# A second buffer for the delta heads' output gates, paid for by a pool of attention constants that ends with the attention

## The chip, the cores and the metric

The kernel runs on one core of a Trainium2 chip: TensorE (PE, with its weight loads PEld), VectorE (DVE), ScalarE (ACT), GpSimd (POOL) and SyncE (SP, which issues most DMAs). The metric is the time of one execution in microseconds, the median of the runs shown. The profile tells of one execution; its span runs from the first to the last instruction.

## The reference

One step of a decoder layer for a prompt of 1024 tokens and 8 single-token samples, in float32. What bears on the change is the gated delta rule with 8 heads of width 128, and its output gate:

```python
h = rmsnorm(x) * (1 + scale1) + shift1
qkv, gdn_gate, beta_raw, a_raw, sq, sk, sv, ga, gb = split(h @ w_in)
q, k, v = silu(causal_conv4(qkv))            # per head 128 wide; q, k normalized
for each chunk of the prompt:                # a chain through the state S
    v_new = u - w @ S
    o     = q_dec @ S + a_intra @ v_new
    S     = S * last + k_dec.T @ v_new
y_a = (rmsnorm(o) * w_norm * silu(gdn_gate)) @ w_gdn_out
y_b = sliding_window_attention(sq, sk, sv) @ w_swa_out
x   = x + gate1 * ((sigmoid(ga) * y_a + sigmoid(gb) * y_b) @ w_o)
x   = x + gate2 * ffn(rmsnorm(x))            # conv-gated feed-forward, 2816 wide
```

Here `u` and `w` come from the inverse of a unit triangular matrix for each chunk, which the kernel forms for each head with 128 tokens in a chunk. The silu(gdn_gate) of each head is the output gate of the title.

## The kernel before

**Stages.** The conditioning and the first norm, the sliding-window attention in four groups, the delta heads one after the other, the branches (`branches`, the output projections of attention and delta heads), and the feed-forward half. Activations lie with features on the partitions and the 1032 tokens along the free dimension, in three parts of 384, 384 and 264 columns. Every product of float32 matrices is made of three fast ones (`mm3`, L180 to L182: high by high, low by high, high by low), over eight steps of 128 features. So a projection of 128 columns for a part is 24 matmuls, and for all tokens 72.

**A delta head.** `run` starts head 0 and then goes through h = 0 to 7. For each h it weaves these streams: `unit_inverse(h)`, the blockwise inverse of head h (in five blocks of small matmuls: L1038, L1044, L1056, L1061, L1070 and, last, L1074, with copies on ScalarE and transposes on VectorE between them); `delta_scan(h)`, eight chunks, each with a chain of products with the key (L947), the inverse W (L950) and the decayed key (L954), between which lie y on VectorE (L948), s on ScalarE (L952) and the new state S on VectorE (L963); `delta_prepare(h + 1)`, transposes and Gram products (L190, L906, L907); and projections. Those are, for h up to 5, `delta_gate(h)` and after it `delta_project(h + 2)`, which makes K, Q and V of the head after the next with `conv_tile`: project, copy into a room z (L780), four taps on VectorE (L784, L786) and a silu (L791, L792). At h = 6 the gates of heads 6 and 7 come in their place.

`delta_gate(h)` projects 72 matmuls, takes the tanh of each part from PSUM on ScalarE (L858) and writes the gate on VectorE into `sg` (L859). The scan multiplies its normalized output into `sg` in two halves (L983) and sends it to DRAM as `oa` (L988). `sg` has one buffer, so the gate of a head can be written only when the output of the head before has left; head 7's takes a room z instead.

**Rooms that matter.** K and Q have three buffers (`bufs=3`), V has one, and z has two, one of them in the pool `pz` and one in `pa`. Projections use two banks of PSUM (`pmm`, tag mm), the filler a third one (`pmf`).

**Filler.** `gates` (the two branch gates, 16 tiles of 72 matmuls, evicted by ScalarE at L1294 into gt) and `early_out` (the attention's output projection for one part of the tokens, evicted at L1326 by VectorE with a gate that is loaded from DRAM at L1323) come in `pieces` of eight steps with a low priority. In the stages of heads 6 and 7 each filler step is also tied to a step of the scan (`spaced`). When the last gate is done, six loads of sample states (L1119, 512 KB each) use the room that it frees.

**What sets the order.** A scheduler places all instructions: `weave` and `later` give priorities, and a simulated timeline tells when an operand, a PSUM bank or a room is ready. Each engine then runs its instructions in that fixed order, and a later tile of a pool waits for the tiles that lay at its addresses.

**Pools.** `cp` holds the constants of the whole program, `cp2` those that last through the branches. `p2`, the attention's pool, ends with it, and `pgt`, `pz`, `pg`, `pa` and `p4` (which has `sg`) take the space then.

Of the kernel before, what the change touches and what calls it, by code (L numbers as in the profile page):

```python
# [18 lines left out]
P = 128  # L19
NP = 1024  # L20
NS = 8
NT = NP + NS
KC = 8
H = 8
# [9 lines left out]
HALF = [(0, 512), (512, 520)]  # L34
QW = 260
KEPT = {"ident", "ones", "mhalf", "phalf", "vecs", "fcw", "mT", "a2"}
COL_GATE, COL_BETA, COL_SQ = 3072, 4096, 4112
COL_SK, COL_SV, COL_GA, COL_GB = 5136, 5392, 5648, 6672

# [25 lines left out]
class Step:  # L65
# [28 lines left out]
        return pool.tile(shape, dt, tag=tag, name=f"{tag}_{self.n}", **kw)  # L94

    def const(self, shape, name, dt=F32):
        pool = self.cp if name in KEPT else self.cp2
        return pool.tile(shape, dt, tag=name, name=name)


# [749 lines left out]
    def delta_gate(self, pa, pool, h):  # L850

        nc = self.nc
        sg = self.t(pool, [P, NT], "sg", bufs=1) if h + 1 < H else self.t(self.pz, [P, NT + 3], "z")[:, :NT]

        def gate_out(t, ps):
            lo, n = PARTS[t]
            th = self.t(pa, [P, 512], "th", bufs=2)[:, :n]
            nc.scalar.activation(th, ps, AF.Tanh, scale=0.5)  # L858
            nc.vector.scalar_tensor_tensor(sg[:, lo:lo + n], th, 1.0, ps, op0=ALU.add, op1=ALU.mult)  # L859

        self.project(self.win(COL_GATE + h * P), self.h, gate_out)
        nc.gpsimd.tensor_copy(self.sgs[:, h, :], sg[:, NP:NT])
        self.sg[h] = sg
        yield
# [1086 lines left out]

    def run(self):
        S, nc = ExitStack, self.nc
        self.constants()
        with S() as ca:
            with S() as c:
                pool, psum = self.pool("p2", 1, ctx=c), self.pool("q2", 1, PSUM, ctx=c)
                for tag, bufs in dict(qst=8, raw=2, kh=2, kl=2, E=3, obt=2, pp=2, pc=2, o=2).items():
                    self.bufs[id(pool), tag] = bufs
                self.conditioning(pool, psum)  # L1960
                self.vectors(pool, psum)
                self.h = self.new_parts()
                self.a1 = self.const([P, KC, 9], "a1")
                for lo in (8, 0, 12, 4):
                    self.modulation(pool, psum, "sc", lo, (("qst", 8),), "mrows")
                    if lo == 8:
                        self.junk = self.t(pool, [P, NP], "vch", bufs=1)
                        xs = self.norm_part(pool, self.load_rows(pool, 0, ("raw", "raw", "V")))
                    if lo in (8, 12):
                        k = lo - 8  # L1970
                        self.norm_scale(self.a1[:, k:k + 4, :], lo, self.n1w[:, k:k + 4])
                    if lo == 0:
                        self.modulate_part(pool, psum, 0, xs, self.a1, 0, range(4))
                    if lo == 12:
                        self.early = [self.win(COL_SK)]
                    if lo == 4:
                        self.early.append(self.win(COL_SQ))
                with self.tc.issue_after(self.mod_load.ins):
                    self.early.append(self.win(COL_SV, tags=("wmh", "wml"), home=pool, raw=(pool, "qst", 8)))
                with self.tc.issue_after(self.w_load.ins):  # L1980
                    self.xs = {1: self.load_rows(pool, 1, ["qst"] * 3)}
                self.junk = self.t(pool, [P, NP], "qst", bufs=8)
                self.early.append(self.win(COL_SQ + P, tags=("obt", "obt"), home=pool))
                self.xs[2] = self.load_rows(pool, 2, ("raw", "raw", "V"))
                self.modulate_part(pool, psum, 0, xs, self.a1, 0, range(4, KC))
                self.attention(pool, psum)
# [6 lines left out]
            with S() as c:  # L1993
                pa, pool, psum = self.pool("pa", 1, ctx=c), self.pool("p4", 1, ctx=c), self.pool("q4", 1, PSUM, ctx=c)
# [27 lines left out]
        with S() as c:  # L2022
            pool2, pool = self.pool("p6b", 1, ctx=c), self.pool("p6", 1, ctx=c)
# [48 lines left out]
```

## Time and profile before

| | us |
|---|---|
| median of 3 runs | 2083.78 |
| lowest and highest | 2079.47, 2090.38 |
| span of the profiled execution | 2084.4 |
| PE busy | 2012.7 (97%) |
| DVE busy | 1347.8 (65%) |
| ACT busy | 900.2 (43%) |
| POOL busy | 520.2 (25%) |
| mean granted TensorE clock | 0.991 |

The profiled execution is known by its span alone, which holds what the times measure; it lies 0.6 us above the median. A row of the profile that groups instructions has the line, engine and operation, the written and read tiles, the count, then the busy time in us and the mean of one in ns, and last the idle time of the engine before them with what ended it. A row of a timeline has the start, the duration, the instruction and in brackets the idle time before it. A row of waits has who waited for whom, the total, how often and the longest. The attention ends at about 440 us, the delta heads at about 1110.

### The profile page before, as it was taken

The page shows a single profiled execution, that of the slowest core. Times are in us where ns is not written, and L with a number is a line of the kernel's source. Part 1 is how long each engine was busy: PE and PEld are TensorE (multiplying, and loading weights), DVE is VectorE, ACT ScalarE, POOL GpSimd, SP SyncE. Part 2 cuts the span into 40 slices and gives each one's busy share as a digit, 9 for nine tenths or more (in the row PEclk, how much of TensorE's full clock was granted, in tenths as well). Part 3 has the DMA queues.
Part 4 walks back from the last instruction along what each step waited for, and adds up shares of the span by engine and source line. Part 5 has one row for each costly group of instructions (what it writes and reads, how often), then busy time and mean ns, then how long its engine had stood idle before and what let it go on. Part 6 is the DMA issues. An engine that isn't in the chain of part 4 may idle for free.

```text
span 2084.4 us, 41297 instructions
## 1 busy us (share of the span) xinstructions
PE 2012.7 (97%) x16245; PEld 1910.2 (92%) x16245; DVE 1347.8 (65%) x2714; ACT 900.2 (43%) x2233; POOL 520.2 (25%) x594
## 2 busy tenths in 40 slices
PE   7999998999999999989989999999999999999897
PEld 4987877799999999989989999999999999999897
DVE  5755768473655647656544675578876776767756
ACT  4664545433344243432342542354444444534443
POOL 2000000121321221201111000005575466446421
PEclk9999999999999999999999999999999999999999
DMA  8256443331332322312275855323333333488862
GB/s 300 62 144 210 135 167 116 117 94 51 80 80 61 73 72 52 89 42 62 63 223 172 285 186 163 112 63 97 105 91 112 102 92 112 136 305 266 291 215 94
DMA packets 301887, 275.75 MB, mean 132 GB/s; under 512 B 59730, under 2 KB 248111, under 8 KB 301676
## 3 DMA queue, kind: packets, MB, share of 16 engines
q1 hardware_dynamic: 295642, 252.14, 39.6%
q0 software_dynamic: 5552, 20.37, 2.8%
q8 instruction: 127, 2.08, 0.4%
q14 instruction: 68, 0.56, 0.1%
q10 hardware_dynamic: 498, 0.61, 0.1%
HBM read 212.93 MB, written 62.51 MB: 132 GB/s over the span
## 4 chain that ended last, share of the span: by engine, by line
PE 83%; DVE 5%; DMA 5%; ACT 3%; issue 1%; SPq 1%; POOL 1%; DVEq 0%; POOLq 0%; ACTq 0%
PE mm L180 19%; PE mm L181 18%; PE mm L182 18%; PE wv L180 3%; PE wv L182 3%; PE wv L181 3%; PE wy L182 2%; PE wy L180 2%; PE wy L181 2%; PE pv L652 1%; PE pt L190 1%; PE tp L190 1%; DVE x L1472 1%; PE mm L264 1%; PE rc L954 1%
## 5 line engine op out<-in xcount | busy, mean ns | idle before, releaser
L180 PE MATMUL mm<-b1h,wh 128*128 128x384 f32 (+1 forms) x1520 | 496.9, 328 | 3.7 <-ACT gt L1294 1.6
L181 PE MATMUL mm<-b1l,wh 128*128 128x384 f32 (+1 forms) x1520 | 489.3, 323 | 0.0
L182 PE MATMUL mm<-b1h,wl 128*128 128x384 f32 (+1 forms) x1520 | 488.0, 323 | 0.3 <-DVE wl L130 0.3
L180 PEld LDWEIGHTS mm<-b1h,wh 128*128 128x128 f32 x1520 | 286.7, 189 | 12.4 <-issue 4.6
L181 PEld LDWEIGHTS mm<-b1l,wh 128*128 128x128 f32 x1520 | 287.1, 189 | 4.4 <-issue 3.1
L182 PEld LDWEIGHTS mm<-b1h,wl 128*128 128x128 f32 x1520 | 286.3, 189 | 3.9 <-issue 2.8
L129 ACT ACTIVATE wh<-raw 128x1024 fp32r<-128x1024 f32 x83 | 87.0, 1049 | 122.4 <-PE mm L181 70.2
L130 DVE TENSOR_TENSOR wl<-raw,wh 128x1024 fp32r<-128x1024 f32 x82 | 101.0, 1233 | 57.2 <-ACT wh L129 55.1
L181 PE MATMUL mm<-pk,w 128*128 128x260 f32 (+1 forms) x440 | 124.8, 284 | 1.1 <-DVE pk L130 1.1
L180 PE MATMUL mm<-pk,w 128*128 128x260 f32 (+1 forms) x440 | 124.8, 284 | 0.0
L182 PE MATMUL mm<-pk,w 128*128 128x260 f32 (+1 forms) x440 | 124.5, 283 | 0.0
L130 DVE TENSOR_TENSOR w<-ws,w 128x512 fp32r<-128x512 f32 x88 | 78.0, 886 | 36.9 <-ACT w L129 36.7
L1626 ACT COPY bml<-mm 128x256 f32<-128x256 f32 (+1 forms) x132 | 48.9, 371 | 100.6 <-PE mm L182 96.7
L180 PE MATMUL mm<-bmh,w 128*128 128x260 f32 (+1 forms) x320 | 90.3, 282 | 0.0
L182 PE MATMUL mm<-bmh,w 128*128 128x260 f32 (+1 forms) x320 | 90.1, 282 | 0.0
L1681 DVE SCALAR_TENSOR_TENSOR fa<-fz,fcw,fa 128x512 f32<-128x512 f32 x88 | 75.2, 874 | 18.2 <-ACT fa L1679 17.9
L180 PE MATMUL mm<-b2h,wh 128*128 128x384 f32 (+1 forms) x256 | 83.2, 328 | 2.9 <-ACT wh L129 2.8
L181 PEld LDWEIGHTS mm<-pk,w 128*128 128x128 f32 x440 | 83.2, 189 | 1.3 <-DVE pk L130 1.3
L181 PE MATMUL mm<-b2l,wh 128*128 128x384 f32 (+1 forms) x256 | 83.6, 327 | 0.4 <-DVE b2l L130 0.4
L180 PEld LDWEIGHTS mm<-pk,w 128*128 128x128 f32 x440 | 83.2, 189 | 0.2 <-ACT bml L1626 0.2
L182 PEld LDWEIGHTS mm<-pk,w 128*128 128x128 f32 x440 | 83.4, 190 | 0.0
L182 PE MATMUL mm<-b2h,wl 128*128 128x384 f32 (+1 forms) x256 | 82.8, 326 | 0.0
(645 smaller groups left out, 5886.2 us busy)
## 6 DMA issues: line engine op xcount, KB each, us to landing
raw<-in_w_in_dram SPq DMA_DIRECT2D x59, 512.0 KB
ws<-in_w_ffn_down_dram SPq DMA_DIRECT2D x55, 256.0 KB
raw<-xd SPq DMA_DIRECT2D x47, 258.0 KB
raw<-in_w_ffn_down_dram SPq DMA_DIRECT2D x47, 256.0 KB
raw<-in_w_ffn_gate_dram SPq DMA_DIRECT2D x22, 512.0 KB
raw<-in_w_ffn_up_dram SPq DMA_DIRECT2D x22, 512.0 KB
qst<-in_w_mod_dram SPq DMA_DIRECT2D x16, 512.0 KB
raw<-in_w_mod_dram SPq DMA_DIRECT2D x16, 512.0 KB
```

The source lines that it names most:

```text
L129: self.nc.scalar.activation(hi, x, AF.Copy)
L130: (eng or self.nc.vector).tensor_tensor(lo, x, hi.bitcast(F32), op=ALU.subtract)
L180: mm(ps, whi, xhi, start=first, stop=False, **kw)
L181: mm(ps, whi, xlo, start=False, stop=False, **kw)
L182: self.last_mm = mm(ps, wlo, xhi, start=False, stop=last, **kw).ins
L190: self.nc.tensor.transpose(out, in_, self.ident[:p, :p])
L264: nc.tensor.matmul(ps[32 * j:32 * j + 32], self.cT[:, k0 + j, :], ws[j // 2][:, j % 2, :], start=k0 == 0, stop=k0 > 0)
L652: nc.tensor.matmul(pv[64 * r:64 * r + 64], V[:, n - back, ch], ps[:, r::2, :], start=back == 0, stop=back == (n > 0))
L954: yield step(nc.tensor.matmul(ds, kd[:, n, :], s, start=True, stop=True))
L1472: nc.vector.scalar_tensor_tensor(x[:, :np_], ps[:, :np_], by[:, j, 8:9], x[:, :np_], op0=ALU.mult, op1=ALU.add)
L1626: self.last_copy = nc.scalar.copy(r[p, i], x[p])
L1681: nc.vector.scalar_tensor_tensor(ai[:, c:e], zi[:, j + c:j + e], col(j), ai[:, c:e], op0=ALU.mult, op1=ALU.add)
```

## The change

Ten constants that only the attention (and what runs beside it) reads go from `cp2` into a new pool `cp1`, opened inside the attention's scope and closed with it: four triangular masks, the sinks, four small tiles of sample queries and keys and values, and the modulation of the first norm. They make up 4.8 KB in each partition. `sg` gets two buffers of 4.1 KB, for all eight heads; head 7's gate no longer takes a room z. Constants are now made behind the opening of that pool.

```diff
 KEPT = {"ident", "ones", "mhalf", "phalf", "vecs", "fcw", "mT", "a2"}
+SHORT = {"triu", "tril", "trilu", "stril", "sink", "qs", "kx", "vx", "zero", "a1"}
...
     def const(self, shape, name, dt=F32):
-        pool = self.cp if name in KEPT else self.cp2
+        pool = self.cp if name in KEPT else self.cp1 if name in SHORT else self.cp2
...
     def delta_gate(self, pa, pool, h):
...
-        sg = self.t(pool, [P, NT], "sg", bufs=1) if h + 1 < H else self.t(self.pz, [P, NT + 3], "z")[:, :NT]
+        sg = self.t(pool, [P, NT], "sg", bufs=2)
...
     def run(self):
         S, nc = ExitStack, self.nc
-        self.constants()
         with S() as ca:
             with S() as c:
+                self.cp1 = self.pool("cp1", 1, ctx=c)
+                self.constants()
```

No instruction is added or taken away on any engine. The order stays as it was up to TensorE's work beside the inverse of head 1, and from the branches on it differs in few places. In between, each gate now stands a scan earlier. Three places show what else moved; line numbers of the changed kernel are one higher than the profile's (L1038 is L1039 there).

Place 1: TensorE at the end of head 4's scan, from its last chunk on. rc, o and S belong to the scan, tp to the inverse of head 5 and to the transposes for head 6; mm is a projection. Before (the key that is transposed is head 6's; the last mm is a piece of head 5's gate):

```order
L958 MATMUL o_9698<-s_9733,A_8916 128x128
L182 MATMUL mm_10286<-b1h_12_150,wl_10255 128x384
L947 MATMUL rc_9742<-S_9739,K_7325 128x128
L957 MATMUL o_9698<-S_9739,Q_7326 128x128
L950 MATMUL rc_9745<-y_9741,W_4535 128x128
L954 MATMUL rc_9749<-s_9747,kd_8864 128x128
L958 MATMUL o_9698<-s_9747,A_8916 128x128
L1074 MATMUL tp_10183<-W_4535,UZ_9991 64x64 x8
L190 MATMUL tp_10876<-ident,K_9341 128x128 x4
L190 MATMUL tp_10887<-ident,K_9341 128x128 x4
L190 MATMUL rc_9764<-ident,vn_8949 128x128 x4
```

Now (mm_10600 is the third part of the value projection of head 7; the filler stands behind it):

```order
L948 MATMUL rc_9746<-S_9743,K_7329 128x128
L958 MATMUL o_9702<-S_9743,Q_7330 128x128
L951 MATMUL rc_9749<-y_9745,W_4539 128x128
L955 MATMUL rc_9753<-s_9751,kd_8868 128x128
L959 MATMUL o_9702<-s_9751,A_8920 128x128
L1075 MATMUL tp_10187<-W_4539,UZ_9995 64x64 x8
L191 MATMUL tp_10880<-ident,K_9345 128x128 x4
L191 MATMUL tp_10891<-ident,K_9345 128x128 x4
L181 MATMUL mm_10600<-b1h_14_155,wh_10544 128x264
L182 MATMUL mm_10600<-b1l_15_156,wh_10544 128x264
L183 MATMUL mm_10600<-b1h_14_155,wl_10545 128x264
```

What moved: head 7's value projection now stands here, behind the key transposes; before, it came in the scan of head 5. On VectorE the same place, from the last y of head 4's scan on. Now (K_10347 and Q_10348 are those of head 7):

```order
L949 SCALAR_TENSOR_TENSOR y_9745<-rc_9746,d_2594,vn_8953 128x128
L785 TENSOR_SCALAR K_10347<-z_10350,cw 128x1024
L785 TENSOR_SCALAR Q_10348<-z_10445,cw 128x1024
L787 SCALAR_TENSOR_TENSOR K_10347<-z_10350,cw,K_10347 128x1024
L787 SCALAR_TENSOR_TENSOR Q_10348<-z_10445,cw,Q_10348 128x1024
L964 SCALAR_TENSOR_TENSOR S_9757<-S_9743,d_2595,rc_9753 128x128
L787 SCALAR_TENSOR_TENSOR K_10347<-z_10350,cw,K_10347 128x1024
L787 SCALAR_TENSOR_TENSOR Q_10348<-z_10445,cw,Q_10348 128x1024
L972 TENSOR_SCALAR so_9633<-so_9633 128x4
L787 SCALAR_TENSOR_TENSOR K_10347<-z_10350,cw,K_10347 128x1024
L787 SCALAR_TENSOR_TENSOR Q_10348<-z_10445,cw,Q_10348 128x1024
L973 SCALAR_TENSOR_TENSOR so_9633<-n_1404_8869,so_9633 128x4
```

Before, head 7's key convolution stood in the scan of head 5, amid the steps (T, tmp) of head 6's inverse:

```order
L1020 TENSOR_REDUCE T_10989<-tmp_11022 128x8
L784 TENSOR_SCALAR K_10343<-z_10346,cw 128x1024
L875 TENSOR_TENSOR G_11933<-G_11933,d_2590 128x1024
L1019 TENSOR_TENSOR tmp_11025<-T_10989,MR_10983 128x8x10
L786 SCALAR_TENSOR_TENSOR K_10343<-z_10346,cw,K_10343 128x1024
L1020 TENSOR_REDUCE T_10989<-tmp_11025 128x8
L963 SCALAR_TENSOR_TENSOR S_10683<-S_10669,d_2592,rc_10679 128x128
L786 SCALAR_TENSOR_TENSOR K_10343<-z_10346,cw,K_10343 128x1024
L1019 TENSOR_TENSOR tmp_11028<-T_10989,MR_10983 128x8x11
```

What moved: both convolutions of head 7 now begin right behind the last step of the scan of head 4, whose buffers they take.

Place 2: TensorE beside the last chunks of head 5's scan and the inverse of head 6. Before, between two blocks of the inverse (mm_11323 is head 6's gate, and mm_11351 its last part):

```order
L1070 MATMUL tp_11175<-MR_11055,UZ_10993 64x64 x2
L950 MATMUL rc_10747<-y_10743,W_4535 128x128
L1070 MATMUL tp_11175<-MR_11055,UZ_10993 64x64 x6
L180 MATMUL mm_11323<-b1h_12_150,wh_11291 128x384
L181 MATMUL mm_11323<-b1l_13_151,wh_11291 128x384
L182 MATMUL mm_11323<-b1h_12_150,wl_11292 128x384
L180 MATMUL mm_11323<-b1h_12_150,wh_11291 128x384
L181 MATMUL mm_11323<-b1l_13_151,wh_11291 128x384
L182 MATMUL mm_11323<-b1h_12_150,wl_11292 128x384
L180 MATMUL mm_11351<-b1h_14_152,wh_11291 128x264
L181 MATMUL mm_11351<-b1l_15_153,wh_11291 128x264
```

Now:

```order
L955 MATMUL rc_10727<-s_10725,kd_9876 128x128
L959 MATMUL o_10704<-s_10725,A_9928 128x128
L1071 MATMUL tp_11179<-MR_11059,UZ_10997 64x64 x8
L948 MATMUL rc_10734<-S_10731,K_8337 128x128
L958 MATMUL o_10704<-S_10731,Q_8338 128x128
L951 MATMUL rc_10737<-y_10733,W_4539 128x128
L955 MATMUL rc_10741<-s_10739,kd_9876 128x128
L959 MATMUL o_10704<-s_10739,A_9928 128x128
L948 MATMUL rc_10748<-S_10745,K_8337 128x128
L958 MATMUL o_10704<-S_10745,Q_8338 128x128
L951 MATMUL rc_10751<-y_10747,W_4539 128x128
L955 MATMUL rc_10755<-s_10753,kd_9876 128x128
```

What moved: the gates of heads 6 and 7, which stood between the blocks, are all ahead of the inverse now.

Place 3: TensorE at the inverse of head 7. Before (mm_11714 and mm_11743 are pieces of the branch gates, rc_11554 to rc_11571 the scan of head 6):

```order
L1038 MATMUL tp_12124<-MR_12121,U_1923_12057 32x32 x13
L950 MATMUL rc_11554<-y_11550,W_4535 128x128
L1038 MATMUL tp_12124<-MR_12121,U_1923_12057 32x32 x19
L180 MATMUL mm_11714<-b1h_14_152,wh_11710 128x264
L181 MATMUL mm_11714<-b1l_15_153,wh_11710 128x264
L182 MATMUL mm_11714<-b1h_14_152,wl_11711 128x264
L180 MATMUL mm_11743<-b1h_10_148,wh_11710 128x384
L181 MATMUL mm_11743<-b1l_11_149,wh_11710 128x384
L182 MATMUL mm_11743<-b1h_10_148,wl_11711 128x384
L954 MATMUL rc_11558<-s_11556,kd_10874 128x128
L958 MATMUL o_11535<-s_11556,A_10926 128x128
L190 MATMUL rc_11564<-ident,vn_10959 128x128 x4
```

Now (rc_11611 closes the scan of head 6, rc_12268 opens that of head 7, mm_12431 is a piece of the attention's output projection):

```order
L191 MATMUL rc_11611<-ident,vn_10963 128x128 x4
L182 MATMUL mm_11910<-b1l_1878_11810,wh_11867 128x264
L183 MATMUL mm_11910<-b1h_1877_11809,wl_11868 128x264
L1039 MATMUL tp_12128<-MR_12125,U_1923_12061 32x32 x32
L1045 MATMUL tp_12163<-T_12120,tmp_12161 32x32 x32
L181 MATMUL mm_12431<-b1h_1877_11809,wh_11903 128x264
L182 MATMUL mm_12431<-b1l_1878_11810,wh_11903 128x264
L183 MATMUL mm_12431<-b1h_1877_11809,wl_11904 128x264
L1057 MATMUL tp_12203<-MR_12125,U_1924_12062 32x32 x16
L1062 MATMUL tp_12205<-T_12120,tmp_12204 32x32 x16
L1071 MATMUL tp_12245<-MR_12125,UZ_12063 64x64 x8
L1075 MATMUL tp_12255<-W_4539,UZ_12063 64x64 x8
```

What moved: the scan of head 6 and the last branch gates are over before this inverse begins, and three matmuls are left among its blocks. From the next row on the order is the same as before.

## The prediction

> **What bounds the kernel now.** I read first the span and the busy times, then stretches of the stage that the change touches, then who waits inside the gaps.
>
> ```profile
> span 2084.4 us, 41297 instructions
> PE 2012.7 (97%) x16245; PEld 1910.2 (92%) x16245; DVE 1347.8 (65%) x2714; ACT 900.2 (43%) x2233; POOL 520.2 (25%) x594
> PE 83%; DVE 5%; DMA 5%; ACT 3%; issue 1%; SPq 1%; POOL 1%; DVEq 0%; POOLq 0%; ACTq 0%
> ```
>
> TensorE is busy for 97% of the span and carries 83% of the chain that ends last. The change adds and removes no matmul, so it can only move TensorE's idle time. The stretches of the delta heads (us, then busy time of PE, PEld, DVE, ACT, POOL with instruction counts, then the granted clock) tell how much there is:
>
> ```profile
> 440.00:550.00 110.00, 110.00 (x914) 108.21 (x913) 63.97 (x138) 36.74 (x96) 30.33 (x37) 1.00 0.30 75
> 550.00:880.00 330.00, 326.84 (x2955) 315.72 (x2954) 196.85 (x426) 125.84 (x377) 64.07 (x91) 1.00 0.27 72
> 880.00:914.00 34.00, 31.19 (x370) 29.36 (x369) 18.06 (x29) 9.53 (x23) 2.37 (x5) 0.95 0.16 38
> 914.00:935.00 21.00, 17.29 (x115) 15.20 (x114) 11.26 (x30) 13.76 (x55) 3.04 (x4) 0.84 0.12 42
> 935.00:1000.00 65.00, 65.00 (x599) 63.60 (x597) 42.40 (x86) 18.55 (x42) 9.49 (x17) 1.00 0.27 69
> 1000.00:1016.00 16.00, 14.24 (x121) 12.60 (x120) 6.26 (x14) 12.76 (x53) 2.32 (x3) 1.00 0.22 71
> 1049.00:1079.00 30.00, 29.01 (x385) 26.47 (x383) 14.21 (x25) 15.65 (x36) 3.11 (x4) 1.00 0.78 223
> 1079.00:1105.00 26.00, 19.24 (x136) 17.76 (x135) 11.91 (x23) 8.27 (x18) 1.01 (x1) 0.93 0.80 235
> ```
>
> Width less PE gives the idle time: 0, 3.2, 2.8, 3.7, 0, 1.8, 1.0 and 6.8 us, 19.2 us in all. That is 0.9% of the span, and the most that the change can win here. The first five heads leave almost nothing.
>
> **What is removed.** A single room for the gate held the eviction of a head's gate projection until the previous head's gated output had been sent off. What this wait cost is in one row (idle time of VectorE before the eviction, and its cause):
>
> ```profile
> L859 DVE SCALAR_TENSOR_TENSOR sg<-th,mm 128x384 f32<-128x384 f32 (+1 forms) x21 | 10.2, 507 | 1.7 <-DMA oa<-sg 1.7
> ```
>
> 1.7 us of VectorE, none of it directly TensorE's. What the single room did besides was to hold the projections of heads 2 to 7 back behind the gates, and so to keep them as filler for the end of each scan. With two rooms the order has each gate a scan earlier, and the convolution projections that follow it move up too. These now meet another limit: K and Q have three buffers, so the convolution of head 7 may not write its key before head 4's scan has read its last one. That wait takes the removed one's place, and the filler that runs early is missing later. The cost is summed over three places, those shown in the order.
>
> **Place 1, the end of head 4's scan: +4 us.** Now head 7's key and query convolutions both start behind the last key product (L947) of head 4. Their rows:
>
> ```profile
> L784 DVE TENSOR_SCALAR K<-z,cw 128x1024 f32<-128x1024 f32 x6 | 4.5, 747 | 0.0
> L784 DVE TENSOR_SCALAR Q<-z,cw 128x1024 f32<-128x1024 f32 x6 | 5.0, 826 | 0.0
> L786 DVE SCALAR_TENSOR_TENSOR K<-z,cw,K 128x1024 f32<-128x1024 f32 x18 | 23.0, 1279 | 0.1
> L786 DVE SCALAR_TENSOR_TENSOR Q<-z,cw,Q 128x1024 f32<-128x1024 f32 x18 | 22.8, 1266 | 0.1
> L792 DVE SCALAR_TENSOR_TENSOR K<-z,K 128x512 f32<-128x512 f32 x12 | 8.0, 680 | 0.7 <-ACT z L791 0.7
> L948 DVE SCALAR_TENSOR_TENSOR y<-rc,d,vn 128x128 f32<-128x128 f32 x55 | 19.1, 346 | 26.8 <-PE rc L947 26.6
> L780 ACT COPY z<-mm 128x384 f32<-128x384 f32 (+1 forms) x55 | 24.1, 438 | 62.1 <-PE mm L182 47.5 <-issue 10.8 <-POOL gt L1295 3.8
> ```
>
> VectorE's order there is y 0.35, K 0.75, Q 0.83, three of each by turns 3.84 + 3.80, one state update 0.35 and two small ones 0.3, then the key's two halves 1.36: 11.6 us. Then the room z of the key is free, ScalarE copies head 7's value projection into it (0.44), and only then has the third part of that projection a PSUM bank. On TensorE it stands directly behind the key transposes, and the other filler behind it. TensorE's own work in that time, from rows of the same place now:
>
> ```profile
> 914.77 0.49 PE L947 MATMUL rc<-S,K 128*128 128x128 f32 x2
> 915.09 0.39 PE L957 MATMUL o<-S,Q 128*128 128x128 f32 x2
> 916.23 0.49 PE L950 MATMUL rc<-y,W 128*128 128x128 f32 x2 [0.75 <-DVE y L948]
> 917.48 0.49 PE L954 MATMUL rc<-s,kd 128*128 128x128 f32 x2 [0.77 <-ACT s L952]
> 917.81 0.39 PE L958 MATMUL o<-s,A 128*128 128x128 f32 x2
> 919.81 1.97 PE L1074 MATMUL tp<-W,UZ 64*64 64x64 f32 x16 [1.61 <-ACT W L1065]
> 921.71 1.97 PE L190 MATMUL tp<-ident,K 128*128 128x128 f32 x8
> ```
>
> 0.71 + 0.49 + 0.72 + 1.97 + 1.97 = 5.9 us out of 0.5 + 11.6 + 0.4 = 12.5: 6.6 us idle at that clock; at the speed of the next head's row below (1.14 for L1074) it is some 8. In place of 3.7 (914 to 935) that is +3 to +4.5; I take +4, as the 2.8 of 880 to 914 (the start of the inverse, late by a DMA) may stay or go: bounds 0 and +6.
>
> **Place 2, the inverse of head 6 beside the rest of head 5's scan: +3.5 us.** Today 935 to 1000 has no idle time, because the late gates and the last value projection stand between the steps. Now they are used up, and the last four steps run bare. From the rows above a bare step takes 1.46 (914.77 to 916.23) + 1.25 (to 917.48) + about 1.0 (state update 0.35 and handovers) = 3.7 us, with 1.9 us of matmuls: 1.8 idle, 7.2 in four. Into this fall the inverse's blocks:
>
> ```profile
> 987.28 0.69 PE L1056 MATMUL tp<-MR,U 32*32 32x32 f32 x32
> 992.15 0.69 PE L1061 MATMUL tp<-T,tmp 32*32 32x32 f32 x32
> 1065.15 1.14 PE L1070 MATMUL tp<-MR,UZ 64*64 64x64 f32 x16
> 1071.68 1.14 PE L1074 MATMUL tp<-W,UZ 64*64 64x64 f32 x16
> ```
>
> two of 0.69 like the shown two, and 1.14 (L1070): about 3.9. So 3.3 to 3.6; bounds 0 (all hidden) and 7.
>
> **Place 3, the inverse of head 7: 0, with 1.5 for a slower clock.** Now its blocks are spread between fillers (1.0 us idle in 1049 to 1079), and the scan that follows stalls 6.8 us:
>
> ```profile
> PE rc L954 <- ACT s L952: 3.2, 2, 1.8
> PE rc L947 <- DVE S L961: 2.1, 1, 2.1
> 1082.31 0.43 DVE L1326 TENSOR_TENSOR gt<-mm,gt 128x264 f32<-128x264 f32 x1 [3.33 <-DMA gt<-sgb]
> 1086.12 1.06 ACT L129 ACTIVATE wh<-raw 128x1024 fp32r<-128x1024 f32 x1 [6.55 <-DMA raw<-in_w_swa_out_dram]
> 1068.36 2.60 SPq L1119 DMA_DIRECT2D b1l<-in_state_gdn_S_dram  x3
> ```
>
> VectorE and ScalarE stand before loads queued among six state loads; these waits end 14.0 and 17.8 us after the first of them is issued. In the changed order all fillers precede the inverse, which then runs nearly alone:
>
> ```profile
> L1040 ACT COPY tmp<-tp 128x256 f32<-128x256 f32 x8 | 2.9, 367 | 7.9 <-PE tp L1038 7.8
> L1046 DVE STREAM_TRANSPOSE MR<-T 128x256 f32<-128x256 f32 x8 | 3.5, 443 | 0.2
> L1058 ACT COPY tmp<-tp 32x256 f32<-32x256 f32 x16 | 5.8, 365 | 9.0 <-PE tp L1056 8.7
> L1071 ACT COPY UZ<-tp 64x512 f32<-64x512 f32 x8 | 4.7, 582 | 8.2 <-PE tp L1070 8.1
> ```
>
> Between its blocks lie 0.37, then three operations of about 0.43, then 0.73, then some 0.8, 0.58 and 0.58: 4.3 us, and nine handovers of about 0.1 make 5. In return the loads arrive during it, and the stalls at 1082 and 1086 (some 4.6 of the 6.8) go. 5 + 2.2 against 7.8 today is nothing; if the same loads hold the inverse, since L1326 and the weight split also stand inside its chain, up to 3 more. I take 0 and add 1.5, as a bare chain of 10 us with half its time idle is what lowered the clock to 0.84 in 914 to 935, which doubles the small blocks there (1.97 against 1.14).
>
> The Trainium skill, "TensorE: Matmul & The Clock Gate", section "Part 1: The HAM clock gate (the "warmup" mystery)", says that the array falls to half rate after an idle window of about 3.4 us and returns after a busy one. The rows agree in kind (0.84, 0.93 and 0.95 stand where TensorE idles, 1.00 elsewhere). By the rule places 1 and 3 would bring up to two such windows each, an estimated 3.4 us lost per place instead of my 1.5 for both, and the sum would be some 5 us higher.
>
> **The rest.** Heads 1 to 4 (550 to 880) have 3.2 us to lose, of which half is the filler's wait for a bank:
>
> ```profile
> PE mm L180 <- ACT gt L1294: 1.6, 4, 0.6
> ```
>
> The filler moves to other places, so I take 1 off; bounds 3 less and 3 more. I cost at nothing the start of the stage (the order up to the second inverse is the same, and 440 to 550 has no idle time; if the new addresses make a first load wait, it costs that wait) and the branches, which keep their order but for a few neighbours changed.
>
> **Sum.** 4 + 3.5 + 0 + 1.5 - 1 = +8 on the profiled 2084.4, so 2092; that execution lies 0.6 above the runs' median, so 2091.
>
> **Rivals.** (a) Covered after all, 2078 to 2087: VectorE is 65% busy, so place 1's convolutions may lie beside work that I call bare, and place 2 cover itself. Places 1 and 2 at their lower bounds leave 2084.4 + 0.5 = 2085. Against it stands the missing filler in the order. (b) Faster: the earlier gates close the holes at 914 to 935 and 1079 to 1105, 10.5 us: 2073. For it speaks that these are the two largest holes; against it, that no projection stands in either now. It decides if both gaps fall under 2 us. (c) Slower beyond doubt: the room of K and Q holds TensorE at each of heads 3 to 6 as at head 7, because value projections stand in its order before other filler: 3 us each in three more heads, 2091 + 9 = 2100; a half-speed clock for two windows at places 1 and 3, as the 0.84 of 914 to 935 shows it for one place, would add 5: 2096. It decides once 550 to 880 idles over 6 us. For it speaks VectorE's burst of 11.6 us at each scan's end; against it, that fillers stand between those value projections. (d) The change does nothing since another room holds the gates anyway: the order excludes it, the gates do move.
>
> **Chances.** The forecast, 2087 to 2094: 0.34; (a) 0.22; (b) 0.09; (c) 0.35. Runs of this kernel spread by 0.5%, so less than 0.5% (10.4 us) cannot be told from no change: faster 0.09; same, which is the forecast and (a), 0.56; slower 0.35. The range takes (a) and most of (c): 2079 to 2104.
>
> **What would show it.** Right: idle time before L181 behind the transposes of head 7's key, ended by ScalarE's copy into z, 5 to 8 us; idle steps in head 5's last four chunks; PE total unchanged; the waits on the gate and state loads in head 7's scan smaller. Wrong: idle in the delta stage under 17 us in all, or a gap that is none of the three places.

## The result, and the profile after

The changed kernel takes 2103.28 us in the median of six runs (2100.47 to 2108.72), against 2085.36 for the kernel before in six runs (2079.47 to 2091.81). The ratio is 1.0087 with an interval of 1.0067 to 1.0106: slower by 0.9%, some 18 us. The profiled execution has a span of 2101.8, 17.4 more than before.

The page of the changed kernel, its first lines and the engines of the chain that ended last:

```profile
span 2101.8 us, 41293 instructions
PE 2019.6 (96%) x16245; PEld 1918.2 (91%) x16245; DVE 1350.6 (64%) x2714; ACT 900.3 (43%) x2233; POOL 529.7 (25%) x594
PE 77%; DMA 8%; DVE 7%; ACT 3%; issue 2%; POOL 1%; SPq 1%; DVEq 0%; POOLq 0%; ACTq 0%
```

TensorE runs the same 16245 instructions, but they take 6.9 us longer, and its share of the chain falls from 83% to 77%.

I compared TensorE at the same work: the start of the inverse of head 1, up to which the order is the same (553.5 before, 555.7 after), and one projection in the branches, behind which both kernels do the same (1151.4 and 1170.9). The views by stretches are cut where a scan ends, from the end of one head's scan to the end of the next. Before (heads 4, 5, 6 and 7 in the second to fifth row; the first is head 3), then the sum over the whole way:

```profile
747.60:832.30 84.70, 84.00 (x759) 81.05 (x757) 52.46 (x111) 31.47 (x94) 15.53 (x23) 1.00 0.25 66
832.30:918.00 85.70, 81.01 (x725) 77.90 (x723) 51.69 (x110) 31.70 (x96) 14.97 (x21) 0.98 0.27 70
918.00:1005.00 87.00, 84.84 (x741) 81.63 (x740) 50.57 (x111) 33.44 (x100) 12.82 (x22) 0.96 0.23 62
1005.00:1066.70 61.70, 58.69 (x584) 54.29 (x582) 35.87 (x97) 24.98 (x83) 11.66 (x17) 1.00 0.37 103
1066.70:1115.60 48.90, 42.14 (x319) 40.42 (x318) 23.54 (x42) 17.70 (x40) 3.19 (x3) 0.97 0.71 203
553.50:1151.40 597.90, 577.52 (x5258) 553.22 (x5258) 340.62 (x740) 222.30 (x645) 99.40 (x146) 0.99 0.32 88
```

The same stretches after:

```profile
773.10:870.30 97.20, 97.20 (x841) 95.34 (x839) 54.97 (x114) 34.36 (x100) 18.99 (x26) 1.00 0.26 68
870.30:948.90 78.60, 77.52 (x704) 74.27 (x703) 46.61 (x106) 28.24 (x90) 14.61 (x19) 0.98 0.25 66
948.90:1025.90 77.00, 63.36 (x582) 59.53 (x581) 47.46 (x108) 29.41 (x91) 16.71 (x18) 0.85 0.24 63
1025.90:1074.30 48.40, 43.68 (x294) 40.67 (x293) 28.49 (x87) 20.55 (x74) 11.55 (x17) 0.92 0.34 94
1074.30:1131.90 57.60, 48.62 (x527) 46.70 (x525) 26.55 (x49) 20.35 (x48) 4.17 (x3) 0.85 0.68 184
555.70:1170.90 615.20, 584.28 (x5258) 563.21 (x5259) 339.70 (x739) 222.50 (x645) 107.51 (x146) 0.96 0.32 86
```

The whole way is 615.2 in place of 597.9: 17.3 us, the entire loss. Width less PE gives 30.9 us idle in place of 20.4, so 10.5 of the 17.3 are idle time; in the other 6.8 the same number of matmuls takes longer (584.28 against 577.52), at a granted clock of 0.96 in place of 0.99. How much of the 6.8 is the clock alone is not separated by any run. The stretches tell where. Up to the end of scan 3 nothing is idle, but the scan ends at 870.3 in place of 832.3: the stage of head 3 is 97.2 us long, since more projections stand in it. Head 5's stage then holds 63.4 us of work in 77.0: 13.6 idle, where 2.2 were.

TensorE at the two holes of that stage, after:

```profile
950.38 1.97 PE L1075 MATMUL tp<-W,UZ 64*64 64x64 f32 x16 [1.10 <-ACT W L1066]
952.28 1.97 PE L191 MATMUL tp<-ident,K 128*128 128x128 f32 x8
957.44 0.59 PE L181 MATMUL mm<-b1h,wh 128*128 128x264 f32 x1 [3.19 <-ACT z L781]
967.72 0.38 PE L907 MATMUL tp<-K 128*128 128x128 f32 x2
1008.86 0.86 PE L1039 MATMUL tp<-MR,U 32*32 32x32 f32 x46 [6.63 <-DVE MR L1035]
1027.39 1.97 PE L1075 MATMUL tp<-W,UZ 64*64 64x64 f32 x16 [1.10 <-ACT W L1066]
1029.29 1.11 PE L191 MATMUL tp<-ident,K 128*128 128x128 f32 x4
```

The first is place 1 as predicted: the value projection waits 3.19 us for ScalarE's copy into z, right behind the key transposes. The second, the largest of all, is the wait of head 6's inverse for its first block. The same steps before:

```profile
921.71 1.11 PE L190 MATMUL tp<-ident,K 128*128 128x128 f32 x4
927.87 0.49 PE L906 MATMUL tp<-K 128*128 128x128 f32 x2
977.63 0.31 PE L1038 MATMUL tp<-MR,U 32*32 32x32 f32 x10
1007.39 0.66 PE L190 MATMUL tp<-ident,K 128*128 128x128 f32 x4
```

From head 6's key transposes to the first block of its inverse it is 55.9 us before and 56.6 after. Between them lie the Gram products (L906, L907), 15 steps on VectorE and two trips through DRAM. That the two numbers agree is a coincidence. The first Gram product stands 6.2 us behind the transposes before, and 15.4 after, where VectorE first works off head 7's convolutions and TensorE head 7's value projection (place 1); the 15 steps then take 22.0 us before and 14.4 after. In the kernel before, the same stretch is 41.7 to 63.3 us for the eight heads. Before, projections filled head 6's 56 us; after, they ran out 6.6 us too soon. From the first block to the key transposes of head 7 it is 29.8 before and 20.4 after, where the blocks run nearly bare. So this head takes 77.0 us from key transposes to key transposes with 63 us of work. In none of the fourteen traces is this distance below 74.4 us, whatever the head.

The removed wait did go. Idle time of VectorE before the gate's eviction, by the view of waits from 440 to 1130 us of the changed kernel (1.7 before):

```profile
DVE sg L860 <- DMA oa<-sg: 0.4, 1, 0.4
```

### The profile page after: what moved, and what is told of

Read it like the earlier page. It is cut to its first block, busy times and chain, and to the rows that moved or that the text cites. A ratio compares the mean times of both kernels' runs of the same rounds, so it can differ in the third digit from the quotient of the medians.

```text
span 2101.8 us, 41293 instructions
## 1 busy us (share of the span) xinstructions
PE 2019.6 (96%) x16245; PEld 1918.2 (91%) x16245; DVE 1350.6 (64%) x2714; ACT 900.3 (43%) x2233; POOL 529.7 (25%) x594
## 4 chain that ended last, share of the span: by engine, by line
PE 77%; DMA 8%; DVE 7%; ACT 3%; issue 2%; POOL 1%; SPq 1%; DVEq 0%; POOLq 0%; ACTq 0%
PE mm L181 17%; PE mm L182 17%; PE mm L183 17%; PE wv L181 2%; PE wv L183 2%; PE wv L182 2%; PE pv L653 1%; DMA ws<-in_w_ffn_down_dram 1%; PE wy L181 1%; PE wy L183 1%; PE wy L182 1%; DMA bmh<-in_w_ffn_down_dram 1%; PE pt L191 1%; DVE pk L131 1%; PE tp L191 1%
## 5 line engine op out<-in xcount | busy, mean ns | idle before, releaser
L181 PE MATMUL mm<-b1h,wh 128*128 128x384 f32 (+1 forms) x1520 | 494.8, 328 | 5.6 <-ACT z L781 3.2
L181 PEld LDWEIGHTS mm<-b1h,wh 128*128 128x128 f32 x1520 | 287.1, 189 | 13.3 <-issue 4.6
L181 PE MATMUL mm<-pk,w 128*128 128x260 f32 (+1 forms) x440 | 124.8, 284 | 0.0
L181 PE MATMUL mm<-bmh,w 128*128 128x260 f32 (+1 forms) x320 | 90.3, 282 | 0.0
L181 PE MATMUL mm<-b2h,wh 128*128 128x384 f32 (+1 forms) x256 | 84.4, 330 | 4.6 <-ACT wh L130 3.1
L181 PEld LDWEIGHTS mm<-pk,w 128*128 128x128 f32 x440 | 83.3, 189 | 0.2 <-ACT bml L1627 0.2
```

Source lines behind the costliest of these rows:

```text
L181: mm(ps, whi, xhi, start=first, stop=False, **kw)
```

## The experiments

All times are medians of 4 to 12 runs; the ratio is to the kernel before, run on the same chip in between, which gave 2088.88 beside the runs 1 to 4, 2083.73 beside 5 to 8 and 2087.33 beside 9 to 12. Width, idle and TensorE's busy time are for the same way as above, from the inverse of head 1 to the branches, in the profiled execution.

| run | ratio (interval) | width | idle | busy |
|---|---|---|---|---|
| before | 1 | 597.9 | 20.4 | 577.5 |
| the change | 1.0087 (1.0067 to 1.0106) | 615.2 | 30.9 | 584.3 |
| 1 pool alone | 1.0002 (0.9989 to 1.0014) | 597.6 | 19.4 | 578.3 |
| 2 gates held | 1.0122 (1.0106 to 1.0138) | 628.5 | 33.0 | 595.5 |
| 3 held, not at place 3 | 1.0134 (1.0116 to 1.0151) | 630.4 | 35.6 | 594.8 |
| 4 states later | 1.0092 (1.0075 to 1.0110) | 621.5 | 33.5 | 588.0 |
| 5 evictions held | 1.0115 (1.0097 to 1.0132) | 618.7 | 28.6 | 590.1 |
| 6 three pieces tied | 1.0130 (1.0111 to 1.0149) | 618.6 | 34.9 | 583.7 |
| 7 eight pieces tied | 1.0123 (1.0105 to 1.0142) | 615.2 | 32.5 | 582.7 |
| 8 tied in scans 4 and 5 | 1.0102 (1.0088 to 1.0116) | 616.2 | 34.4 | 581.8 |
| 9 gates 3, 4 released | 1.0018 (1.0009 to 1.0027) | 602.5 | 23.3 | 579.2 |
| 10 gates 5, 6 released | 1.0006 (0.9994 to 1.0018) | 598.1 | 21.5 | 576.6 |
| 11 gates 6, 7 released | 0.9988 (0.9978 to 0.9999) | 597.2 | 20.4 | 576.8 |
| 12 before, states later | 1.0010 (0.9997 to 1.0022) | 597.0 | 20.2 | 576.8 |

**1. The pool alone.** The changed kernel with the gate's buffer and head 7's room as before:

```diff
-        sg = self.t(pool, [P, NT], "sg", bufs=2)
+        sg = self.t(pool, [P, NT], "sg", bufs=1) if h + 1 < H else self.t(self.pz, [P, NT + 3], "z")[:, :NT]
```

> The short constants get their pool that ends with the attention, but the gate keeps its single buffer and head 7's gate its room z, so every engine's order is that of the kernel before; only addresses differ. Order theory (the loss comes from the gates standing a scan earlier): no change, 2085 within 4 us, idle of TensorE in 550 to 1105 us about 19 as before. Placement rival (the new pool or the moved addresses cost something, as the 2.6 us by which the changed kernel is already behind at 60 us suggests): 2090 to 2103.

2088.30 us, no change. Every engine has the order of the kernel before, only addresses differ, and the time is the same. So the new pool and the moved constants cost nothing; the loss comes with the second buffer. The 2.6 us by which the changed kernel's profile lies behind at 60 us are no part of it either: run 12, which has the first kernel's order through the attention and far beyond, is 2.4 behind there too.

**2. Gates held.** The changed kernel, with the matmuls of each gate ordered behind a step of the scan before (gates 1 to 6 behind chunk 5, gate 7 behind chunk 1 of scan 6):

```diff
-        self.project(self.win(COL_GATE + h * P), self.h, gate_out)
+        with self.tc.issue_after(self.chunk[HOLD[h]]) if h in HOLD else nullcontext():
+            self.project(self.win(COL_GATE + h * P), self.h, gate_out)
...
+HOLD = {1: (0, 5), 2: (1, 5), 3: (2, 5), 4: (3, 5), 5: (4, 5), 6: (5, 5), 7: (6, 1)}
```

> The changed kernel with both buffers, but the matmuls of each gate are ordered behind a step of the scan before: gates 1 to 6 behind chunk 5 of scan h-1, gate 7 behind chunk 1 of scan 6. This puts the projections back as cover where the single buffer had left them. Order theory: 2085 within 5 us, so nearly all of the 17 us come back, and the mean clock returns to 0.99. Rival that the second buffer itself or its addresses cost: stays at 2100 to 2105. If the removed wait was worth something of its own: 2080 or less.

2114.99 us: a miss, worse than the change itself. The row of the way:

```profile
552.10:1180.60 628.50, 595.46 (x5272) 571.31 (x5266) 341.73 (x740) 221.04 (x642) 105.19 (x144) 0.96 0.31 84
```

and its waits for the inverses' first blocks (total, how often, longest):

```profile
PE tp L1039 <- DVE MR L1035: 7.1, 3, 4.7
```

The inverses still wait for their first blocks (7.1 us at three of them). The order shows why this was no restoration: a gate that is free from chunk 5 on takes the projections behind it along. 72 and 25 matmuls of head 7's K and Q stand between the last key product of scan 4 and the first of scan 5 (L955), where the first kernel has none of them, and are missing later in scan 5.

**3. Held, but gate 7 only behind scan 5,** so that head 7's inverse runs alone behind scan 6 as in the changed kernel:

```diff
-HOLD = {1: (0, 5), 2: (1, 5), 3: (2, 5), 4: (3, 5), 5: (4, 5), 6: (5, 5), 7: (6, 1)}
+HOLD = {1: (0, 5), 2: (1, 5), 3: (2, 5), 4: (3, 5), 5: (4, 5), 6: (5, 5), 7: (5, 7)}
```

> As the run before it, but gate 7 is held only behind the end of scan 5, so it is used up before the inverse of head 7, which then runs after scan 6 as in the changed kernel (place 3), while places 1 and 2 have their cover back. Order theory by the idle times and slow clock of the changed trace: place 3 is worth about 8 us (3.6 idle, 2.2 in what follows, the rest clock), so 2093 within 4. If all of the loss is at place 2: 2085. If the loss is at place 3 alone: 2103.

2116.01 us, against 2114.99: place 3 made no difference that can be told here. With run 2 as far off as it is, the size that I had read for place 3 from the changed trace (8 us) is not supported; run 11 measures it better.

**4. States later.** The changed kernel, with the six loads of sample states ordered behind the last load of the turned blocks of head 7's inverse:

```diff
-                self.load_state(i, states[i // 3])
+                with self.tc.issue_after(self.turned.ins):
+                    self.load_state(i, states[i // 3])
```

> The changed kernel, with the six loads of sample states ordered behind the last load of the turned blocks of head 7's inverse, in SyncE's queue. In the changed trace that round trip took 14 us (from the first store of T at 1071.9 to the transpose at 1086.0) against 6.5 before, with three state loads issued in the middle of it. If these loads hold the inverse: the round trip falls to about 7 us and the time to about 2097. Rival (the inverse is late by VectorE's splits of the attention output ahead of its rows, and the loads only move into scan 7): no change, 2100 to 2106.

2109.57 us, ratio 1.0092 against 1.0087: no change. In the changed kernel the trip of the blocks through DRAM stands around these loads, and ends with VectorE's transpose at 1086.02:

```profile
1071.94 2.41 SPq L1026 DMA_DIRECT2D wd<-T  x4
1075.98 2.31 SPq L1120 DMA_DIRECT2D b1l<-in_state_gdn_S_dram  x3
1078.56 3.27 SPq L1029 DMA_DIRECT2D T<-wd  x4
1086.02 0.45 DVE L1035 STREAM_TRANSPOSE MR<-T 128x256 f32<-128x256 f32 x1 [2.58 <-DMA T<-wd]
```

That is 14.1 us. With the states later:

```profile
1073.21 1.93 SPq L1026 DMA_DIRECT2D wd<-T  x4
1078.90 1.80 SPq L1029 DMA_DIRECT2D T<-wd  x4
1084.14 0.45 DVE L1035 STREAM_TRANSPOSE MR<-T 128x256 f32<-128x256 f32 x1 [1.70 <-DMA T<-wd]
```

10.9 us. The order is not quite the one intended: one of the six loads is still issued inside the trip (at 1076.97 us), the others behind it. Three loads in the trip go with 14.1 us, one with 10.9, and 6.5 were measured before with none; the time does not follow.

**5. Evictions held.** Closer to what the single buffer did: VectorE's eviction of each gate (heads 1 to 6) stands behind the last product with the gate of the head before, so the gate keeps its PSUM banks until that scan has ended. Gate 7's matmuls stand behind chunk 1 of scan 6.

```diff
-            nc.vector.scalar_tensor_tensor(sg[:, lo:lo + n], th, 1.0, ps, op0=ALU.add, op1=ALU.mult)
+            with self.tc.issue_after(self.out[h - 1]) if h in HOLD else nullcontext():
+                nc.vector.scalar_tensor_tensor(sg[:, lo:lo + n], th, 1.0, ps, op0=ALU.add, op1=ALU.mult)
```

> The changed kernel with both buffers, but VectorE's eviction of each gate (heads 1 to 6) is ordered behind the last product with the gate of the head before (L984), so that the gate keeps its PSUM banks until the scan before has ended, as the single buffer made it, without the wait for the DMA; gate 7's matmuls stand behind chunk 1 of scan 6. The runs that held only the gates' matmuls came out at 2115, since the K, Q and V projections went ahead of the held gates and were missing later. Bank theory (the single buffer ordered everything because a gate that can't be evicted holds the projections' two banks, so that K, Q, V of the head after the next wait too): 2086 within 6. If it is the second buffer's rooms that cost: 2100 or more. If any order but the first one is bad because each hole moves: 2095 to 2115.

2107.45 us: not restored, though this order gives each scan much the same projections as before. The filler is spread differently: scan 4 has 28 matmuls of it in place of 70, since more of it runs in scans 2 and 3. Its row of the way:

```profile
555.30:1174.00 618.70, 590.12 (x5258) 566.33 (x5259) 338.29 (x740) 223.02 (x645) 96.31 (x146) 0.91 0.32 86
```

8.2 us more idle time and 12.6 more matmul time than before. Which of the remaining differences of order makes it, I did not find out.

**6, 7 and 8. Filler tied to the scans.** The changed kernel with the pieces of filler of late stages tied to the steps of their scans, as those of heads 6 and 7 are: three pieces in scan 5 (run 6), eight in scan 5 and one less in each stage before (run 7), six in each of scans 4 and 5 (run 8). Run 6 is one condition:

```diff
-            if h + 2 >= H:
+            if h >= 5:
                 self.steps.append(ins.ins)
```

> The changed kernel with one condition altered: the three pieces of filler of head 5's stage are tied to the steps of scan 5, as the fillers of heads 6 and 7 are. The order then has filler and gate 6 and 7 beside the last chunks of scan 5 and the inverse of head 6. Theory that place 2 is a lack of cover: its 8.8 us more of idle time and some 3 us of slow clock come back, 2093 within 5, with the hole of 6.6 us ahead of the inverse of head 6 below 2. Rival (the hole only moves to the end of scans 3 and 4, which lose this filler): 2100 or more, with new idle time before 960 us.

> As the run before it, with eight pieces tied to scan 5 in place of three and one piece less in each of the stages of heads 0 to 4. In this order gates 6 and 7 fall into scan 6 and part of the inverse of head 7 stands beside that scan, so that places 2 and 3 both have cover. Cover theory: 2086 within 6. Rival (the early scans, short of filler, go bare): idle time in 700 to 940 us rises by 8 or more and the time stays at 2095 to 2105.

> Six pieces tied to scan 4 and six to scan 5, fewer in the stages before. Scan 4's end and scan 5 both have filler, but gate 7 is used up before scan 6's second half and most of the inverse of head 7 stands alone. Cover theory: places 1 and 2 repaired, place 3 partly: 2091 within 6. Rival as in the run before it: 2100 or more.

2109.86, 2109.52 and 2105.39 us: the cover theory fails three times, and the rival holds in runs 6 and 8. In run 7 the early idle time came as the rival said (16.5 us in 700 to 940, where the changed kernel has none and the first kernel 7.9), but the time lies above its range. The hole ahead of head 6's inverse goes (in run 6 the waits of L1039 are 1.9 us in all), but the idle time is 34.9, 32.5 and 34.4. The waits of TensorE in run 6:

```profile
PE mm L181 <- ACT z L781: 7.0, 2, 3.5
PE rc L191 <- DVE vn L977: 4.8, 1, 4.8
PE tp L1039 <- DVE MR L1035: 1.9, 1, 1.9
```

and in run 8:

```profile
PE rc L191 <- DVE vn L977: 10.9, 2, 6.9
PE mm L181 <- ACT z L781: 7.6, 2, 4.1
```

The hole of place 1 now stands at two scan ends, and a new one in the middle of scan 5 (in run 8 also behind scan 7), where TensorE waits for the normalized output. In these three orders, cover taken from one stage left a hole in another.

**9, 10 and 11. One gate at a time.** These three turn the question round. They are the kernel of run 1 with one head's gate in a second buffer of its own, for k = 3, 5 and 6:

```diff
-        sg = self.t(pool, [P, NT], "sg", bufs=1) if h + 1 < H else ...
+        sg = self.t(pool, [P, NT], "sg2" if h in (k,) else "sg", bufs=1) if h + 1 < H else ...
```

Gates k and k+1 are then free of the scan before, and all others are held as in the first kernel, so that the order comes back to the first kernel's some time after.

> The kernel before with the constants' new pool, and only head 3's gate in a second buffer; so the gates of heads 3 and 4 aren't held by the scan before, all others are. The order differs from the first kernel's from the end of scan 2 to the end of scan 4 alone, and is the same behind that. Pacing theory (projections drawn forward must be missing somewhere later, and the harm is done only where no filler is left, at the last heads): no change, 2085 within 4. Rival (each early release leaves a hole of its own at a scan's end, by K's and Q's rooms or z): 2089 to 2095.

> The same with head 5's gate in the second buffer, so gates 5 and 6 are not held. The order is the first kernel's up to the middle of scan 4; behind it, the last value projection and gates 6 and 7 are used up before the last chunks of scan 5 and the inverses of heads 6 and 7 stand bare, as in the changed kernel. Pacing theory: nearly the whole loss, 2098 to 2106, with the idle time at the inverse of head 6. Rival (the loss adds up over all heads): a third of it, 2088 to 2093.

> The same with head 6's gate alone in the second buffer; the order differs only from the end of scan 5 on, where gate 7 is begun earlier and the inverse of head 7 runs alone behind scan 6 (place 3 of the changed kernel, without places 1 and 2). By the changed trace place 3 cost 3.6 us of idle time, some 2 behind it and some 3 of slow clock: 2092 within 4. By the prediction (the waits on the loads vanish in return): 2086.

Run 9 is slower by 0.18% (2091.74), run 10 no different (2088.10), run 11 faster by 0.12% (2084.30), at the edge of what can be told. By my theory (harm only where no filler is left, at the last heads) run 9 was to cost nothing; it costs 4.4 us, within its rival's range. Run 10 was to cost nearly the whole loss and cost none, but its order is not the one I expected and does not test the theory. It has place 3 and the bare last steps of scan 5, but not place 2's want of work. The stage of head 5 in run 10:

```profile
926.20:1011.00 84.80, 83.64 (x737) 80.79 (x735) 53.44 (x114) 31.77 (x95) 16.14 (x20) 0.96 0.26 70
```

It has 737 matmuls (741 before, 582 in the changed kernel) and 1.2 us idle (2.2 and 13.6), although in run 10 head 6's first block comes 63.8 us behind its key transposes, later than in the other two. So it is the amount of other work in the stage that differs here, and not the length of the chain. The stage of head 3 in run 9, where the gates come early, and of head 4 behind it:

```profile
749.50:847.50 98.00, 98.00 (x847) 96.13 (x845) 56.30 (x115) 35.92 (x103) 19.55 (x25) 1.00 0.24 64
847.50:920.80 73.30, 65.90 (x612) 61.95 (x611) 44.68 (x102) 26.77 (x87) 15.44 (x20) 0.94 0.26 67
920.80:1155.70 234.90, 220.96 (x1946) 209.95 (x1945) 125.43 (x284) 84.27 (x240) 32.69 (x49) 0.98 0.43 121
```

Head 3's stage is as long as in the changed kernel (98.0 and 97.2), but the stage behind it gives most of that back: 73.3 in place of 85.7. Run 10 from the end of scan 4 on, and the same part of the kernel before and of the changed one:

```profile
926.20:1151.60 225.40, 209.26 (x1857) 200.29 (x1856) 123.55 (x280) 81.03 (x233) 36.58 (x47) 0.93 0.44 123
```

```profile
918.00:1151.40 233.40, 220.55 (x1944) 209.72 (x1944) 125.51 (x284) 84.49 (x241) 32.96 (x50) 0.98 0.43 122
```

```profile
948.90:1170.90 222.00, 192.17 (x1705) 181.71 (x1705) 118.19 (x276) 78.68 (x230) 37.71 (x46) 0.89 0.44 122
```

Run 10 is 8.2 us late at the end of scan 4 and gives back 8.0. The changed kernel is 30.9 late there (28.7 without the difference of the start), and gives back 11.4: 17.3 are lost. Its last three heads have 28 us less work than before, but need 222 us all the same. Run 9 counted from the end of scan 3 is 15.2 late and gives back 10.9. So a lead of 8 us cost nothing, one of 15 cost 4, and one of 29 cost 17. The three are not counted at the same scan, and no common limit follows from them: counted from the end of scan 3, as for run 9, the changed kernel is 35.8 us late and gives back 18.5.

Run 11 has place 3 alone: the inverse of head 7 behind scan 6. It costs nothing.

**12. The kernel before, with the states later:** the six loads of states stand behind the fourth load of a branch gate in SyncE's queue.

```diff
-            if i < 6:
-                self.load_state(i, states[i // 3])
...
+            if i == 3:
+                with self.tc.issue_after(behind.ins):
+                    for n in range(6): self.load_state(n, states[n // 3])
```

> The kernel before, with the six loads of sample states ordered in SyncE's queue behind the fourth load of a branch gate (L1323), instead of ahead of the first two. In the trace of before the scan of head 7 stalled 6.8 us behind loads queued among them. If the queue is the cause: 2 to 5 us faster, 2081, the waits on S L961 and s L952 in that scan below 2 us together. If the stall has another cause: no change. If the states are then late for the branches, slower by what they wait there.

2088.08 us, no change. TensorE's waits from 1079 to 1120 us:

```profile
PE rc L954 <- ACT s L952: 3.9, 2, 3.2
PE mm L180 <- ACT wh L129: 1.7, 1, 1.7
```

The wait for the state S is gone, but that for s stays at 3.9 (3.2 before), and the weights' split now makes TensorE wait 1.7. The queue was only a part of that stall.

None of these versions clearly beats the kernel before.

## Why the prediction was right in its range and wrong in its size

The time, 2103.3, lies in the stated range (2079 to 2104), at its upper edge, and slower had a chance of 0.35. The likeliest case (2087 to 2094, +8 us) did not come true: the loss is 17.3 us on the same way.

- **Place 1: the mechanism was right, the sum was not.** TensorE stalls before L181 behind the key transposes until ScalarE has copied into z, 5.4 us in 930 to 960 with the bare steps ahead. But it takes the place not only of the 3.7 us in 914 to 935 that I set against it, but of the 2.8 at 880 to 914 too, which I had left open: 6.5 went and 5.4 came, -1.1 in place of +4. The wait for z itself is 3.19 us, below the 5 to 8 named as a sign.
- **Place 2: the step that failed.** I summed the bare steps and blocks, 3.5 us, and took it that the inverse begins when they do. In 1000 to 1033 TensorE idles 10.6 us, where 1.8 were in 1000 to 1016 and none before: +8.8. Without the 6.63 before the first block (MR L1035) 4.0 are left, near the 3.5; the missing term is the 6.63. I never set the time from the key transposes to that block (55.9 us in the profile of before) against the work left to fill it, since nothing waited there while filler covered it. Nor did I ask what else place 1's burst on VectorE would hold up: head 6's Gram products come 9.2 us later behind the transposes. That the hole would close without this delay was not tested.
- **Place 3: 0 by the prediction.** Run 11, which has it alone, measures no cost. In the changed kernel the stages of heads 6 and 7 together idle 13.7 us in place of 9.8; head 6's stage has 294 matmuls in place of 584. VectorE's wait for the gate loads (gt) fell as predicted, from 5.4 to 1.9.
- **Heads 1 to 4: -1.** They lost all their idle time, -3.2. This small gain is where the loss is made: the stages of heads 1 to 3 take 92 to 97 us in place of 85 to 88 because they do more. Counted by stages, the 10.5 us are 11.5 more in that of head 5, 3.9 more in those of heads 6 and 7, 1.6 more behind scan 7, and 6.5 less ahead of them.
- **The clock: 1.5.** The matmuls took 6.8 us longer, where an unchanged total was a sign of being right. The stretch around place 1, after (pieces of 3.4 us):

```profile
938.50:941.90 3.40, 3.40 (x50) 2.83 (x48) 0.55 (x3) 0.52 (x2) 0.00 (x0) 1.00 0.02 5
941.90:945.30 3.40, 2.86 (x55) 2.40 (x54) 0.95 (x3) 0.94 (x3) 0.00 (x0) 1.00 0.00 0
945.30:948.70 3.40, 2.87 (x13) 2.16 (x12) 2.36 (x4) 1.62 (x4) 0.00 (x0) 0.50 0.00 0
948.70:952.10 3.40, 2.30 (x19) 2.00 (x18) 3.40 (x5) 3.13 (x13) 0.93 (x1) 0.50 0.07 19
952.10:955.50 3.40, 2.15 (x11) 1.60 (x9) 3.40 (x5) 1.73 (x3) 0.00 (x0) 0.50 0.00 0
955.50:959.00 3.50, 1.56 (x7) 1.57 (x8) 2.60 (x7) 3.30 (x14) 2.58 (x2) 0.50 0.03 7
959.00:962.40 3.40, 3.40 (x17) 3.32 (x17) 1.88 (x3) 1.33 (x8) 0.00 (x0) 0.50 0.00 0
```

The clock is at half for 17.1 us here. The prediction had put the price of a bare chain's clock at 1.5 for places 1 and 3 together, and 5 more in rival (c). By the rule of the Trainium skill, "TensorE: Matmul & The Clock Gate", section "Part 1: The HAM clock gate (the "warmup" mystery)", as the prediction weighed it, the sum would have been some 5 us higher, 2097. The 6.8 us are nearer to that than to the 1.5.

- **The rivals.** (a) and (b) are excluded: the idle time rose by 10.5. (c), put at 2096 to 2100, came nearest to the time, in part by the wrong mechanism: K's and Q's rooms were to hold TensorE at the heads before, and to show in 550 to 880 as more than 6 us idle; there it is 0.0. Its other half, the clock, has about the right size if the 6.8 us are the clock's. (d) is excluded by the run of the pool alone against the change.

What is shown is that the loss comes with the second buffer (run 1 against the change), and that the largest part of the idle time stands in the stage of head 5, which has 582 matmuls in place of 741. My reading is that the second buffer took away a pace. With one buffer a gate waits for the scan before, and the projections behind it wait too, which keeps the stages of heads 1 to 5 at 85 to 88 us each, with 81 to 87 of work. With two, projections come earlier at every head, scan 3 ends 36 us later (counted from the same start), and less work is left for the heads behind it than the 74 us or more that pass from key transposes to key transposes.

This reading is not shown by giving the pace back. Runs 2 and 5 were made for that and lost as much as the change or more. In run 5 the lead is only 12.0 us at the end of scan 3 and 5.4 at the end of scan 4, and the way is still 20.8 us longer, so a large lead is not needed for the loss; why runs 2, 3 and 5 to 8 lose as much stays open. So does what sets these 74 us: the stretch from key transposes to first block varies from head to head, and no run shortens it. More buffers for K and Q were not tried, for want of space.

## What to carry to other kernels

A wait in a profile may be a pace: the 1.7 us of VectorE before the gate's eviction were no loss to TensorE, and without the order that stood behind them the kernel is 18 us slower. Before giving a resource a second buffer, look at what becomes free to run early, and whether the stages behind it still have as much independent work as their own dependent chain is long; that length is to be read from start to start in the trace, also where nothing waits now, and for several heads, since one of them is not a rule (41.7 to 63.3 us here). A change that frees all heads need not be the sum of changes that free a few: the releases tried (gates 3 to 7) cost -3 to +4 us each and 2 together, all of them 18; gates 1 and 2 were not freed alone.

## What the runs showed of the hardware

**A half clock that followed a busy TensorE.** In the rows above the first piece at half clock (945.3) follows one in which TensorE is busy for 2.86 of 3.40 us, with 55 matmuls, most of them blocks of the inverse; the piece before that is busy throughout. The same section of the Trainium skill has the gate fall after an idle window of about 3.4 us. The 17.1 us at half clock are five such lengths, but no idle window stands ahead of them here.

**A granted clock of 0.95 that cost nothing.** In the profiled execution of run 5 the granted clock is 0.95 wherever it is not half, also where TensorE is busy without a gap. Run 5, then run 1, from 1500 to 1900 us:

```profile
1500.00:1900.00 400.00, 400.00 (x3359) 400.00 (x3358) 289.84 (x473) 182.95 (x345) 222.18 (x229) 0.95 0.41 133
```

```profile
1500.00:1900.00 400.00, 400.00 (x3359) 400.00 (x3358) 295.84 (x460) 183.04 (x340) 225.60 (x222) 1.00 0.45 143
```

Both do 3359 matmuls in these 400 us. I have no explanation; the mean granted clock of an execution is therefore no measure of its time.
